# Expert routing of a one-core hybrid layer: a softmax for each head, gathers inside the routing, and a 16-bit look-up

## The chip, the cores and the metric

The kernel runs on one core of one Trainium2 chip. The metric is the device time of one execution in microseconds. Of several executions the median is taken. TensorE is PE in the profile (its weight loads PEld), VectorE is DVE, ScalarE is ACT, GpSimd is POOL and SyncE is SP.

## The reference

One layer works on 512 tokens of width 1024 with 256 context tokens. A first half (adaLN, RMSNorm, an input projection, an S5 scan and a Hyena convolution, an output projection, a gated residual) is not touched by the change. The second half is PEER, product-key retrieval of single-neuron experts. Each of 8 heads scores 128 + 128 half keys, takes the best 16 of each half, adds them in pairs, and takes the best 16 of the sums:

```python
v1, i1 = lax.top_k(s1, 16)
v2, i2 = lax.top_k(s2, 16)
cand = (v1[..., :, None] + v2[..., None, :]).reshape(..., 256)
sc, ci = lax.top_k(cand, 16)
e = take_along_axis(i1, ci // 16) * 128 + take_along_axis(i2, ci % 16)
g = jax.nn.softmax(sc, axis=-1)
act = jax.nn.gelu(einsum('chkd,cd->chk', take(u_tab, e), hb))
out = einsum('chk,chkd->cd', g * act, take(v_tab, e))
```

So each token has 8 x 16 = 128 experts e out of 16384, each with a gate g. `x + gate * out` and a final RMSNorm are the output. All data are float32.

## The kernel before, in words

The 512 tokens are served in two ways. The first 128 tokens (`NG`) are served by **gathers**: `gathered(s)` (lines 1428 to 1439) fetches for slot s (one of the 128 head-and-rank slots) each token's expert row, u and v side by side, 1 MB in all, by an indirect DMA on POOL's queue (line 1430, index column `gidx[:, s]`) into one of three buffers `uvr` (`NUV`). DVE then multiplies u with the token's row and sums (line 1431, the dot product), ACT takes the gelu of the dot (line 1434) and multiplies by the gate `gt0[:, s]` (line 1436), and DVE adds gate times v to `accg` (line 1439). The other 384 tokens (`ND`) are served **densely**: all 128 tiles of 128 experts are computed for all these tokens. For tile i, `first(i)` (lines 1360 to 1370) loads the u weights, splits them into a high part (ACT, line 302) and a low part (DVE, line 303), runs 24 matmuls of 384 columns and takes the gelu. `second(i)` (lines 1602 to 1631) loads the v weights `vr` (512 KB), splits them in the same way (`vh` on ACT, line 1611; `vl` on DVE, line 1612), multiplies the stored gelu `gal` by the stored gates `gc` (DVE, line 1617), splits the product (lines 1620 and 1621) and runs 18 matmuls of 512 columns into `pacc`.

Every dense product is three float32r matmuls (high x high, high x low, low x high: `mm3`, lines 306 to 309).

The stages in order of time, behind the untouched first half:

1. **Routing**, the loop over the 8 heads (lines 1465 to 1490): two query projections of 24 matmuls (`pq`), the scores of four token blocks (`psc`, line 1483), the best 16 of each half (`top16`, lines 1346 to 1352, on DVE), and `pairs` (lines 1382 to 1419). `pairs` adds the 54 candidate sums and, beside them, the 54 expert numbers (`ca`; `NCAND` = 54), takes the best 16 of the sums, and looks their expert numbers up: for each of four token blocks, line 1416 compares the 16 found positions with 0..53 (a 128 x 16 x 54 mask), line 1417 multiplies the mask by the 54 numbers, and line 1418 sums over the 54 to give `EID`. All three are DVE instructions on float32. Behind each head, `run_ahead(RH)` places `first` for 6.3 tiles on average, whose results go to DRAM (`GA`): they fill PE while DVE sorts. Once, behind all heads, `softmax(None)` (lines 1443 to 1455) makes the gates of all heads with one ACT exponential, and writes `gidx` and `gt0`, which the gathers need.
2. **Gates** (lines 1567 to 1590): `columns` and `gates` turn expert numbers and gates into dense gate rows for the 384 tokens, in 96 groups of four tokens, with four small matmuls a group (`pgg`). Behind each group, `gathers(G_SHARE)` adds 0.23 gathers and `run_ahead(RG)` adds 0.34 tiles. `run_ahead(RS)` puts 4 tiles ahead of it, and `run_ahead(NRUN)` the rest, up to `NRUN` tiles, behind it.
3. **The second loop** (lines 1638 to 1643): `second(i)` for all 128 tiles. For i under `NRUN` nothing else runs on PE; from there on, `first` of one tile goes with each `second`. The remaining gathers are spread over this loop by the factor `left` (line 1635), so many for an i under `NRUN` times `R_RUN`, and so many for each later i.

`gathers(share)` adds up shares and issues `gathered` whenever the sum passes a whole number; its first DVE instruction is kept behind the instruction passed as `after`. A scheduler that works from estimated times orders the instructions of each engine at build time; on the chip each engine and each DMA queue then runs strictly in that order.

Of the kernel before, what the change touches and what calls it, by code (L numbers as in the profile page):

```python
# [11 lines left out]
I32 = mybir.dt.int32  # L12
BF16 = mybir.dt.bfloat16
U32 = mybir.dt.uint32
AF = mybir.ActivationFunctionType
ALU = mybir.AluOpType
AX = mybir.AxisListType

P = 128
# [52 lines left out]
          ("bglu", 4), ("gs5", 4), ("ghy", 4), ("negt", 4), ("a_re", 32), ("a_im", 32), ("lstep", 32))  # L72
NG = 128
SG = 32
NRUN = 91
NUV = 3
G_SHARE = 0.23
R_RUN = 0.4
ACT_OH = (2,1)
RG = 0.34  # L80
RH = 6.3
RS = 4
EQ_POOL = 3
G_LAG = 3
# [7 lines left out]
QUIET = 1  # L92
WGT_ACT = 1
RGATE = 0
PERHEAD = 0
GH = 2.0
NOO = 3
S5M = 1
HYAT = 2
# [5 lines left out]
NCAND = 54 if MERGE else 50  # L105
# [123 lines left out]
def build(tc, I, out, dbg=None, stop=None):  # L229
# [58 lines left out]
    def b2(name, shape, dtype=F32):  # L288
        return cur[0].tile(shape, dtype, tag="b2", name=name, bufs=nb2[0])
# [4 lines left out]
    def sm(name, shape, dtype=F32, bufs=1, tag=None):  # L294
        return cur[0].tile(shape, dtype, tag=tag or name, name=name, bufs=bufs)

    def wblock(src, name, lo_eng=None):
# [3 lines left out]
        lo = wp.tile([P, D], F32R, tag="wl", name=name + "l")  # L301
        nc.scalar.activation(hi, raw, AF.Copy)
        (lo_eng or (nc.vector if FQ else nc.gpsimd)).tensor_tensor(lo, raw, hi.bitcast(F32), ALU.subtract)
# [30 lines left out]
    V = nc.vector  # L334
    A = nc.scalar
# [83 lines left out]
    sc = cp.tile([P, 8, 2], F32, tag="sc", name="sc")  # L419
    A.activation(sc, ccs, AF.Silu)  # L420
    mod = cp.tile([P, 48], F32, tag="mod", name="mod")
# [15 lines left out]
    def modulated(name, rows, n, scale_c, shift_c, put, ks):  # L437
        for k in ks:
# [3 lines left out]
            hi, lo = put(k)  # L442
            A.activation(hi, pp[:, :n], AF.Identity, bias=shift_c[:, k:k + 1], scale=scale_c[:, k:k + 1])
            t = b2(f"{name}t{k}", [P, 512])[:, :n]
# [3 lines left out]
    def root_sums(n, name, ps_, diag, nb=4):  # L448
# [9 lines left out]
        def inverse(scale):  # L458
            c4 = cp.tile([P, 4], F32, tag="c4", name=name + "4", bufs=2)
            A.activation(c4[:, 0:nb], pc_[:, 0:nb], AF.Sqrt, bias=epsc, scale=scale)  # L460
            V.reciprocal(c4[:, 0:nb], c4[:, 0:nb])
# [8 lines left out]
    def row_sums(n, name, ps_, tmp, width=512):  # L470
# [4 lines left out]
        def add(t, eng=None):  # L475
            i = at[0]
            at[0] += 1
            hi, lo = (tmp(f"{name}{c}{i}", F32R)[:, 0:width] for c in "hl")
            A.activation(hi, t, AF.Copy)
            (eng or V).tensor_tensor(lo, t, hi.bitcast(F32), ALU.subtract)  # L480
# [3 lines left out]
        def inverse(scale, o, view=lambda t: t):  # L484
            root = tmp(name + "q", F32)[:, 0:width]
            A.activation(root, pc_, AF.Sqrt, bias=epsc, scale=scale)
            V.reciprocal(o, view(root))
# [848 lines left out]
    gate[0] = None  # L1336
    iota50 = sm("iota50", [P, NCAND])
    GP.iota(iota50, pattern=[[1, NCAND]], base=0, channel_multiplier=0, allow_small_or_imprecise_dtypes=True)
    iotak = sm("iotak", [P, P])
    GP.iota(iotak, pattern=[[1, P]], base=0, channel_multiplier=0, allow_small_or_imprecise_dtypes=True)  # L1340
    gt0 = rt("gt0", [P, P])
# [2 lines left out]
    EID = sm("EID", [P, 4, 8, 16])  # L1344

    def top16(val, idx, src, n, name):
        V.max(val[:, 0:8], src)
        V.max_index(idx[:, 0:8], val[:, 0:8], src)  # L1348
        rest = sm(name, [P, 128], tag="rest", bufs=4)[:, :n]
        V.match_replace(rest, val[:, 0:8], src, NEG)  # L1350
        V.max(val[:, 8:16], rest)
        V.max_index(idx[:, 8:16], val[:, 8:16], rest)  # L1352
# [4 lines left out]

    GA = dram.tile([NRUN, P, ND], F32, name="GA")

# [15 lines left out]
    def run_ahead(share):  # L1375
        ran[0] += share
        while ran[1] < min(NRUN, ran[0]):
            i = ran[1]
            ran[1] += 1
            nc.scalar.dma_start(GA[i], first(i, V if QUIET else GP))  # L1380

    def pairs(hd, val, idx):

        if MERGE:
            V.tensor_copy(val[:, :, 4:8], idx)
            V.tensor_scalar(val[:, 0, 4:8], val[:, 0, 4:8], float(P), None, ALU.mult)
            ca = sm(f"ca{hd}", [P, 8, NCAND], tag="cand", bufs=2)
            cand, cid = ca[:, 0:4], ca[:, 4:8]
            at = 0
            for (i0, m, n) in RECTS:  # L1390
                V.tensor_tensor(ca[:, :, at:at + m * n].rearrange("p w (i j) -> p w i j", j=n), val[:, 1, :, 0:n].unsqueeze(2).broadcast_to((P, 8, m, n)),
                                val[:, 0, :, i0:i0 + m].unsqueeze(3).broadcast_to((P, 8, m, n)), ALU.add)
                at += m * n
        else:
            idf = sm(f"idf{hd}", [P, 2, 4, 16], tag="idf", bufs=2)
            V.tensor_copy(idf, idx)
            V.tensor_scalar(idf[:, 0], idf[:, 0], float(P), None, ALU.mult)
            cand = sm(f"cand{hd}", [P, 4, NCAND], tag="cand", bufs=2)
            cid = sm(f"cid{hd}", [P, 4, NCAND], tag="cid", bufs=2)
            at = 0  # L1400
            for i in range(9):
                n = 16 // (i + 1) if i < 8 else 8
                for (dst, s) in ((cand, val), (cid, idf)):
                    if i < 8:
                        V.tensor_tensor(dst[:, :, at:at + n], s[:, 1, :, 0:n], s[:, 0, :, i:i + 1].broadcast_to((P, 4, n)), ALU.add)
                    else:
                        V.tensor_tensor(dst[:, :, at:at + n], s[:, 0, :, 8:16], s[:, 1, :, 0:1].broadcast_to((P, 4, n)), ALU.add)
                at += n
        pos = sm(f"pos{hd}", [P, 4, 16], U32, tag="pos", bufs=2)
        for lt in range(4):  # L1410
            top16(SC[:, lt, hd], pos[:, lt], cand[:, lt], NCAND, f"rc{hd}{lt}")
        posf = sm(f"posf{hd}", [P, 4, 16], tag="posf", bufs=2)
        V.tensor_copy(posf, pos)
        for lt in range(4):
            eq = sm(f"eq{hd}{lt}", [P, 16, NCAND], tag="eq", bufs=2)
            V.tensor_tensor(eq, posf[:, lt].unsqueeze(2).broadcast_to((P, 16, NCAND)), iota50.unsqueeze(1).broadcast_to((P, 16, NCAND)), ALU.is_equal)
            (GP if not QUIET and lt < EQ_POOL else V).tensor_tensor(eq, eq, cid[:, lt].unsqueeze(1).broadcast_to((P, 16, NCAND)), ALU.mult)
            last = V.tensor_reduce(EID[:, lt, hd], eq, AX.X, ALU.add)
        return last
# [23 lines left out]
    def softmax(hd):  # L1443
        h_ = slice(hd, hd + 1) if hd is not None else slice(0, 8)
        n = 1 if hd is not None else 8
        sc, gx = SC[:, :, h_], GX[:, :, h_]
        V.tensor_tensor(gx, sc, sc[:, :, :, 0:1].broadcast_to((P, 4, n, 16)), ALU.subtract)
        A.activation(gx, gx, AF.Exp)
        gsum = sm(f"gsum{hd}", [P, 4, 8], tag="gsum", bufs=2)[:, :, 0:n]
        V.tensor_reduce(gsum, gx, AX.X, ALU.add)  # L1450
        V.reciprocal(gsum, gsum)
        V.tensor_tensor(gx, gx, gsum.unsqueeze(3).broadcast_to((P, 4, n, 16)), ALU.mult)
        c_ = slice(16 * h_.start, 16 * h_.stop)
        V.tensor_copy(gidx[:, c_], EID[:, 0, h_].rearrange("p h k -> p (h k)"))
        V.tensor_copy(gt0[:, c_], GX[:, 0, h_].rearrange("p h k -> p (h k)"))
# [3 lines left out]
    def gathers(share, after):  # L1459
        due[0] += share  # L1460
        while due[1] < min(P, due[0]):
            gathered(due[1], after)
            due[1] += 1

    for hd in range(8):
# [12 lines left out]
        val = sm(f"val{hd}", [P, 2, 8 if MERGE else 4, 16], tag="val", bufs=2)  # L1478
        idx = sm(f"idx{hd}", [P, 2, 4, 16], U32, tag="idx", bufs=2)
        for lt in range(4):  # L1480
# [5 lines left out]
        last = pairs(hd, val, idx)  # L1486
        if PERHEAD:
            softmax(hd)
            gathers(GH if hd else 0, last)
        run_ahead(RH)  # L1490

# [77 lines left out]
    for e in range(2):  # L1569
# [5 lines left out]
        A.activation(gx2[:, e * 512:(e + 1) * 512], pgx, AF.Copy)  # L1575
    if not PERHEAD:
        softmax(None)
# [7 lines left out]
    for lt in range(1, 4):  # L1585
        if RGATE:
            cols_lt = columns(lt, eids[:, lt], gts[:, lt])
        for b_ in range(P // SG):
            (gates_r if RGATE else gates)((lt - 1) * (P // SG) + b_, cols_lt if RGATE else cols[lt - 1], b_ * SG)
    run_ahead(NRUN)  # L1590
    fr.close()
# [42 lines left out]
    nc.sync.dma_start(gfin, I["g_final"].broadcast_to((P, D)))  # L1634
    left = (P - due[1] - N_SLACK) / (R_RUN * NRUN + (P - NRUN))
    ready = {}
    made = NRUN
    for i in range(P):
# [3 lines left out]
        last = second(i, ready.pop(i, None))  # L1642
        gathers(left * (R_RUN if i < NRUN else 1.0) if i < P - 1 else P, last)

# [58 lines left out]
```

## Time and profile before

| what | us |
|---|---|
| median of three runs | 1772.52 |
| the three runs | 1772.52, 1769.88, 1780.96 |
| the profiled execution, its own time | 1780.91 |
| its span (first to last instruction) | 1779.1 |
| mean granted TensorE clock in it | 0.977 of full speed |

The span is 1.8 us shorter than the execution's own time. A profile's busy time is that of one engine; matmuls are pipelined, so that the distance between the starts of two equal matmuls says more than the duration of one.

### The profile page before, as it was taken

The numbers are of one execution on the slowest core, as the hardware profiler recorded it, in microseconds if no ns is written. First come the engines' busy times: TensorE is split into PE (matmuls) and PEld (weight loads), VectorE is DVE, ScalarE is ACT, GpSimd is POOL, SyncE is SP. The second block draws the span as 40 slices with busy tenths as digits, with TensorE's granted clock in tenths as the row PEclk, the third lists the DMA queues.
The fourth block names the chain that finished last, engine by engine and source line by source line (L and its number), as shares of the span: only waits on it lengthen the run. The fifth ranks groups of instructions, "written<-read, shape, count | busy, mean of one in ns | idle before, by whom it ended". The sixth has DMA issues, their size and how long they took to land.

```text
span 1779.1 us, 24951 instructions
## 1 busy us (share of the span) xinstructions
PE 1669.7 (94%) x8731; PEld 1410.9 (79%) x8731; DVE 1489.1 (84%) x3031; ACT 817.7 (46%) x1622; POOL 165.5 (9%) x158
## 2 busy tenths in 40 slices
PE   5799998788899999999999999989999999999997
PEld 1477655365699999999999998877778778999996
DVE  7964988986788989989999966888878888788888
ACT  3443543134443223326999864443434434444444
POOL 0000000000000000001111100111111112121222
PEclk9899999898899999999999999999999999999998
DMA  9426454131434444445988899999999999999982
GB/s 373 155 88 211 162 163 101 48 75 63 136 123 149 137 146 145 145 142 214 345 330 316 320 346 380 381 384 372 364 338 377 369 349 326 329 325 353 338 322 96
DMA packets 171092, 437.31 MB, mean 246 GB/s; under 512 B 17235, under 2 KB 102868, under 8 KB 151766
## 3 DMA queue, kind: packets, MB, share of 16 engines
q1 hardware_dynamic: 129286, 251.87, 41.8%
q0 software_dynamic: 18432, 134.23, 20.1%
q10 hardware_dynamic: 23248, 49.62, 7.8%
q8 instruction: 69, 1.13, 0.3%
q14 instruction: 57, 0.47, 0.1%
HBM read 382.11 MB, written 53.51 MB: 245 GB/s over the span
## 4 chain that ended last, share of the span: by engine, by line
PE 63%; DVE 12%; DMA 1%; issue 1%; ACT 1%; SPq 0%; DVEq 0%; ACTq 0%
PE pacc L307 10%; PE pacc L308 10%; PE pacc L309 9%; PE pa L309 6%; PE pa L307 6%; PE pa L308 6%; PE pgg L1560 5%; PE pq L309 2%; PE pq L307 2%; PE pq L308 2%; DVE idx L1352 1%; DVE rs L1350 1%; PE pg L1266 1%; DVE idx L1348 1%; DMA GD<-gst 1%
## 5 line engine op out<-in xcount | busy, mean ns | idle before, releaser
L308 PE MATMUL pacc<-vl,wwh 128*128 128x512 f32 x768 | 299.2, 390 | 0.3 <-DVE vl L1612 0.3
L309 PE MATMUL pacc<-vh,wwl 128*128 128x512 f32 x768 | 292.8, 390 | 0.0
L1430 POOL DMA_INDIRECT uvr<-in_uv_dram,gidx x128 | 153.2, 1197 | 1092.1 <-DVE accg L1439 764.2
L307 PE MATMUL pacc<-vh,wwh 128*128 128x512 f32 x768 | 241.0, 393 | 13.7 <-ACT vh L1611 13.7
L1612 DVE TENSOR_TENSOR vl<-vr,vh 128x1024 fp32r<-128x1024 f32 x128 | 155.5, 1220 | 33.3 <-ACT vh L1611 33.1
L307 PEld LDWEIGHTS pacc<-vh,wwh 128*128 128x128 f32 x768 | 144.2, 189 | 45.6 <-ACT vh L1611 16.9
L308 PEld LDWEIGHTS pacc<-vl,wwh 128*128 128x128 f32 x768 | 144.3, 188 | 30.5 <-DVE vl L1612 0.7
L309 PEld LDWEIGHTS pacc<-vh,wwl 128*128 128x128 f32 x768 | 144.2, 188 | 30.0
L1439 DVE SCALAR_TENSOR_TENSOR accg<-uvr,wgt,accg 128x1024 f32<-128x1024 f32 x128 | 163.7, 1279 | 4.5 <-ACT wgt L1436 1.9
L1611 ACT ACTIVATE vh<-vr 128x1024 fp32r<-128x1024 f32 x128 | 133.2, 1049 | 53.5 <-PE pacc L309 39.9
L1431 DVE SCALAR_TENSOR_TENSOR junk<-uvr,hrow 128x1024 f32<-128x1024 f32 x128 | 155.9, 1218 | 0.0
L1620 ACT ACTIVATE wwh<-gw 128x384 fp32r<-128x384 f32 x128 | 67.1, 524 | 183.0 <-PE pacc L308 152.1
L1621 DVE TENSOR_TENSOR wwl<-gw,wwh 128x384 fp32r<-128x384 f32 x128 | 70.8, 555 | 51.8 <-ACT wwh L1620 51.8
L1560 PE MATMUL pgg<-o,o 128*128 128x128 f32 x768 | 94.6, 275 | 0.0
L1560 PEld LDWEIGHTS pgg<-o,o 128*128 128x128 f32 x768 | 93.7, 191 | 0.0
L1551 DVE TENSOR_TENSOR o<-iotak,cols 128x512 f32<-128x512 f32 x96 | 65.9, 687 | 7.8 <-PE pgg L1560 7.6
L1434 ACT ACTIVATE wgt<-dots 128x1 f32<-128x1 f32 x128 | 25.4, 198 | 102.4 <-DVE junk L1431 102.4
L1558 DVE TENSOR_SCALAR o<-iotak,cols 128x128 f32<-128x128 f32 x240 | 70.5, 345 | 0.0
L1556 ACT ACTIVATE o<-o,cols 128x128 f32<-128x128 f32 x144 | 63.8, 494 | 0.2
L1369 ACT ACTIVATE ga<-pa 128x384 f32<-128x384 f32 x128 | 60.6, 474 | 6.0 <-PE pa L309 4.5
L1562 ACT ACTIVATE gst<-pgg 128x512 f32<-128x512 f32 x96 | 57.0, 594 | 3.1 <-PE pgg L1560 2.5
L1617 DVE TENSOR_TENSOR gw<-gal,gc 128x384 f32<-128x384 f32 x91 | 50.0, 553 | 3.4 <-DMA gal<-GA 2.8
(1811 smaller groups left out, 4136.3 us busy)
## 6 DMA issues: line engine op xcount, KB each, us to landing
vr<-in_uv_dram SPq DMA_DIRECT2D x128, 512.0 KB
GD<-gst ACTq DMA_DIRECT2D x12, 2048.0 KB
gc<-GD SPq DMA_DIRECT2D x32, 768.0 KB
GA<-ga ACTq DMA_DIRECT2D x91, 192.0 KB
gal<-GA SPq DMA_DIRECT2D x91, 192.0 KB
wb<-in_w_ada_dram SPq DMA_DIRECT2D x32, 512.0 KB
wa<-in_w_ada_dram SPq DMA_DIRECT2D x8, 1024.0 KB
KD<-kk SPq DMA_DIRECT2D x16, 256.0 KB
```

Source lines behind the costliest of these rows:

```text
L307: nc.tensor.matmul(o, a[0], b[0], start=start, stop=False)
L308: nc.tensor.matmul(o, a[0], b[1], start=False, stop=False)
L309: nc.tensor.matmul(o, a[1], b[0], start=False, stop=stop_)
L1430: GP.indirect_dma_start(out=uvr, out_offset=None, in_=I["uv"], in_offset=bass.IndirectOffsetOnAxis(ap=gidx[:, s:s + 1], axis=0))
L1431: ins = V.scalar_tensor_tensor(junk, uvr[:, 0:D], 1.0, hrow, ALU.mult, ALU.mult, accum_out=dots[:, s:s + 1])
L1439: V.scalar_tensor_tensor(accg, uvr[:, D:2 * D], wgt[:, s:s + 1], accg, ALU.mult, ALU.add)
L1558: last = V.tensor_scalar(o1[:, e], iotak, cols[:, 0, t:t + 1], cols[:, 2, t:t + 1], ALU.is_equal, ALU.mult)
L1560: mm = PE.matmul(pg[:, e, :], o2[:, e], o1[:, e], start=True, stop=True)
L1611: A.activation(vh, vr, AF.Copy)
L1612: (V if QUIET or i >= P - VLV else GP).tensor_tensor(vl, vr, vh.bitcast(F32), ALU.subtract)
L1620: A.activation(wh, gw, AF.Copy)
L1621: last = V.tensor_tensor(wl, gw, wh.bitcast(F32), ALU.subtract)
```

## The change

- `PERHEAD` = 1: `softmax(hd)` runs for each head inside the routing loop, on 4 x 16 scores a token instead of 4 x 8 x 16, and writes that head's 16 columns of `gidx` and `gt0`. The call behind the loop goes.
- `GH` = 3: behind each head but the first, three gathers are placed in the routing loop.
- `PAIR16` = 1: the look-up of `pairs` works on 16-bit types. ACT makes a bf16 copy of the positions, spread out to 16 x 54 (`posx`), and an int16 copy of the expert numbers (`cid16`); DVE compares bf16 with bf16 into int16, multiplies int16 by int16, and sums int16 to float32.
- `NRUN` 91 to 96, `RH` 6.3 to 7, `R_RUN` 0.4 to 0.35.

```diff
-NRUN = 91
+NRUN = 96
-R_RUN = 0.4
+R_RUN = 0.35
-RH = 6.3
+RH = 7
-PERHEAD = 0
-GH = 2.0
+PERHEAD = 1
+GH = 3.0
+PAIR16 = 1
...
+    iota16 = sm("iota16", [P, NCAND], BF16)
+    A.activation(iota16, iota50, AF.Copy)
...
         posf = sm(f"posf{hd}", [P, 4, 16], tag="posf", bufs=2)
         V.tensor_copy(posf, pos)
+        if PAIR16:
+            cid16 = sm(f"cid16{hd}", [P, 4, NCAND], I16, tag="cid16", bufs=2)
+            A.activation(cid16, cid, AF.Copy)
+            for lt in range(4):
+                posx = sm(f"posx{hd}{lt}", [P, 16, NCAND], BF16, tag="posx", bufs=2)
+                A.activation(posx, posf[:, lt].unsqueeze(2).broadcast_to((P, 16, NCAND)), AF.Copy)
+                eq = sm(f"eq{hd}{lt}", [P, 16, NCAND], I16, tag="eq", bufs=2)
+                V.tensor_tensor(eq, posx, iota16.unsqueeze(1).broadcast_to((P, 16, NCAND)), ALU.is_equal)
+                V.tensor_tensor(eq, eq, cid16[:, lt].unsqueeze(1).broadcast_to((P, 16, NCAND)), ALU.mult)
+                last = V.tensor_reduce(EID[:, lt, hd], eq, AX.X, ALU.add)
+            return last
         for lt in range(4):
```

The loop over the heads had the two calls already, behind `if PERHEAD` (lines 1487 to 1489): `softmax(hd)` and `gathers(GH if hd else 0, last)`.

## Rows read from the trace of the kernel before

**Rows 1.** The page, first part: busy time of each engine in the span
```profile
PE 1669.7 (94%) x8731; PEld 1410.9 (79%) x8731; DVE 1489.1 (84%) x3031; ACT 817.7 (46%) x1622; POOL 165.5 (9%) x158
```

**Rows 2.** Windows: stretch; busy us (count) of PE, PEld, DVE, ACT, POOL; clock, DMA share, GB/s
```profile
510.00:825.00 315.00, 312.52 (x1726) 296.36 (x1725) 283.96 (x988) 101.18 (x137) 4.23 (x3) 1.00 0.46 151
825.00:835.00 10.00, 8.79 (x57) 8.28 (x57) 9.05 (x26) 8.64 (x25) 0.00 (x0) 1.00 0.94 383
...
1160.00:1460.00 300.00, 286.05 (x1246) 233.62 (x1245) 251.57 (x338) 121.69 (x225) 51.27 (x43) 0.99 1.02 366
1460.00:1766.00 306.00, 306.00 (x1523) 275.21 (x1522) 252.84 (x318) 132.71 (x258) 59.80 (x51) 1.00 0.85 306
```

**Rows 3.** Windows, one head of six tiles, then one of seven
```profile
549.15:587.42 38.27, 37.98 (x210) 35.71 (x209) 35.19 (x125) 11.72 (x17) 0.00 (x0) 1.00 0.44 145
...
625.69:668.26 42.57, 42.16 (x234) 39.93 (x233) 36.41 (x125) 13.15 (x19) 0.00 (x0) 1.00 0.45 148
```

**Rows 4.** Timeline of DVE, where a head begins (start, duration, idle before)
```profile
668.26 0.52 DVE L1347 MAX8 val<-psc 128x8 f32<-128x128 f32 x2 [2.99 <-PE psc L1483]
```

**Rows 5.** Groups by form, DVE, 440 to 860 us, then its end alone (busy us, mean ns)
```profile
L1416 DVE TENSOR_TENSOR eq<-posf,iota 128x864 f32<-128x864 f32 x32 | 32.6, 1050 | 0.3
L1418 DVE TENSOR_REDUCE EID<-eq 128x16 f32<-128x864 f32 x32 | 32.3, 1040 | 0.0
L1417 DVE TENSOR_TENSOR eq<-eq,ca 128x864 f32<-128x864 f32 x32 | 32.3, 1049 | 0.0
...
L1391 DVE TENSOR_TENSOR ca<-val 128x64 f32<-128x64 f32 x2 | 0.4, 220 | 0.0
```

**Rows 6.** Timeline of DVE in the first half: an instruction with one full operand
```profile
402.57 0.48 DVE L1199 TENSOR_SCALAR catz<-x2t,small 128x512 f32<-128x512 f32 x1
```

**Rows 7.** Groups by form, DVE: gates, then the second loop up to 1460 us
```profile
L1551 DVE TENSOR_TENSOR o<-iotak,cols 128x512 f32<-128x512 f32 x93 | 63.8, 687 | 7.7 <-PE pgg L1560 7.6
...
L1439 DVE SCALAR_TENSOR_TENSOR accg<-uvr,wgt,accg 128x1024 f32<-128x1024 f32 x53 | 67.8, 1280 | 2.5 <-ACT wgt L1436 0.6
L1431 DVE SCALAR_TENSOR_TENSOR junk<-uvr,hrow 128x1024 f32<-128x1024 f32 x53 | 64.5, 1218 | 0.0
...
L1617 DVE TENSOR_TENSOR gw<-gal,gc 128x384 f32<-128x384 f32 x88 | 48.3, 553 | 3.4 <-DMA gal<-GA 2.8
```

**Rows 8.** Waits of PE, routing, 510 to 825 us (the longest of eight)
```profile
PE pa L309 <- DVE u44l L303: 0.4, 1, 0.4
```

**Rows 9.** Timeline of ACT around the one softmax
```profile
806.18 1.28 ACT L1448 ACT_TABLE_LOAD   x1
...
807.48 0.63 ACT L1448 ACTIVATE GX<-GX 128x512 f32<-128x512 f32 x1
```

**Rows 10.** Timeline of PE in the second loop, starts of two iterations
```profile
1160.36 1.52 PE L307 MATMUL pacc<-vh,wwh 128*128 128x512 f32 x6
...
1164.44 1.52 PE L307 MATMUL pacc<-vh,wwh 128*128 128x512 f32 x6
```

**Rows 11.** Waits of PE, 1160 to 1460 us (total, times, longest)
```profile
PE pacc L307 <- ACT vh L1611: 13.7, 7, 3.6
```

**Rows 12.** Windows of the second loop, columns as in rows 2
```profile
1200.00:1300.00 100.00, 93.61 (x409) 76.24 (x409) 85.61 (x116) 39.53 (x76) 18.60 (x16) 0.99 1.02 364
1300.00:1400.00 100.00, 98.40 (x428) 80.53 (x427) 82.60 (x112) 40.89 (x75) 17.30 (x14) 0.99 0.99 362
1400.00:1500.00 100.00, 98.67 (x444) 82.30 (x443) 84.77 (x112) 43.07 (x79) 17.00 (x15) 1.00 0.97 342
```

**Rows 13.** The page: POOL's queue (packets, MB, share), then sizes of DMA issues
```profile
q0 software_dynamic: 18432, 134.23, 20.1%
...
vr<-in_uv_dram SPq DMA_DIRECT2D x128, 512.0 KB
...
gc<-GD SPq DMA_DIRECT2D x32, 768.0 KB
...
gal<-GA SPq DMA_DIRECT2D x91, 192.0 KB
```

More of the change, by code (lines that the diff above doesn't have):

```diff
@@ L14 @@
 U32 = mybir.dt.uint32
+I16 = mybir.dt.int16
 AF = mybir.ActivationFunctionType
```

## The prediction

> **What bounds the kernel now.** I read the page first: PE is busy for 94% of the span, DVE for 84% [rows 1]. Such shares are averages, so next come the windows by stage [rows 2]. PE is busy for 312.52 of 315 us in the routing and for all of 306 us in the last part of the second loop. The stretches with idle time that the change can reach are three: 2.5 us in the routing, 1.2 us at the change to the gates, and 14.0 us (300 - 286.05) between 1160 and 1460 us of the second loop. Nothing in the change removes a matmul. So what it can win is that idle time, some 17.7 us of 1779 or 1.0%, and what it can lose is new idle time of PE in the routing, where DVE gets more to do.
>
> The windows of single heads say how near DVE is to being the bound there [rows 3]. A head with six tiles takes 38.27 us and one with seven 42.57, with PE busy but for 0.3 to 0.4 us in both: a tile costs 4.30 us of PE, and a head lasts as long as its PE work. DVE is idle for 6.16 us of a seven-tile head (42.57 - 36.41), 2.99 of them in a single wait for the next head's scores [rows 4].
>
> In the second loop the waits name one cause for PE: seven waits for `vh`, 13.7 us in all [rows 11]. An iteration without `first` takes 4.08 us (1164.44 - 1160.36) [rows 10]. It moves 512 KB of `vr`, 192 KB of `gal` and a quarter of 768 KB of `gc` [rows 13], 0.918 MB, and its part of a gather of 134.23 / 128 = 1.049 MB [rows 13]. With 23 gathers placed before the loop (96 groups x 0.23, rounded up), `left` is (128 - 23 + 7) / (0.4 x 91 + 37) = 1.526, so 0.610 gathers an iteration: 1.558 MB in 4.08 us, or 382 GB/s. The windows show 1.02 as DMA share in this part and 0.85 in the last part, where PE never waits [rows 2]. The loop is thus held by PE and, for its first 91 iterations, by the DMA engines as well.
>
> **The change, part by part.** *Five more tiles ahead.* 6.3 x 8 = 50.4, so 51 tiles in the routing, become 56; `first` leaves the second loop five times (37 to 32). At 4.30 us a tile the routing gets 21.5 us longer and the loop 21.5 us shorter: no net effect while PE stays busy. The last three tiles behind the gates stay three (88 to 91 before; 92.64 is rounded up to 93, then 96). The five added splits take DVE time in the routing and give it back in the loop; a seven-tile head [rows 3] holds them already.
>
> *Three gathers a head.* 7 x 3 = 21 gathers move ahead. Each costs DVE 1.218 + 1.280 us [rows 7], so 7.5 us a head. DMA has room in the routing: 151 GB/s at a share of 0.46 [rows 2], and three gathers in 42.57 us add 74 GB/s. Their transfers need not be late: once two heads have written 32 columns of `gidx`, three buffers can be filled well before DVE wants them. Behind a gather that waits for its column or its buffer POOL has only gathers; SP's queue is passed by none of the moved work, and ACT's issues five more stores of 192 KB.
>
> *Softmax by head.* Six small DVE instructions a head. On 64 numbers the nearest row takes 0.22 us [rows 5]: 1.3 us a head, with 0.8 (if the shorter ones are cheaper) and 2 as bounds. On ACT each head adds two table loads of 1.28 us [rows 9], a short exponential, four spread copies of 864 elements (0.63 us for 512 [rows 9], so at most 1.06 in proportion; I take 0.95) and the small ones of three gathers: some 8 us, where ACT is busy for 13.15 of 42.57 us [rows 3]. This is covered as long as ACT's in-order queue does not hold up a tile's high part.
>
> The table load is where a rule speaks against the change. The row shows the exponential starting 1.30 us after the load's start [rows 9]. The Trainium skill (ScalarE: Activation LUTs, What ACT_TABLE_LOAD costs) puts a switch of table sets at about 2.66 us, since a drain follows the load; 16 switches would then be 43 us of ACT in place of 21. The trace does not show the drain at this place.
>
> *The look-up in 16 bits.* The compare and the multiply take 1.05 us each, four times a head [rows 5]. No row shows a 16-bit operand on DVE. If time goes by elements, the cost stays 1.05; if by bytes, 864 elements of two bytes are 1728 bytes a partition, between the rows of 384 and 512 float32 elements, 0.553 and 0.687 us [rows 7]: about 0.60. Both rows are equally near. I take 0.60, because one row shows that bytes count: 512 elements with one full operand take 0.48 us [rows 6], with two 0.687 [rows 7]. That saves 8 x 0.45 = 3.6 us a head; the sum stays at 1.04. The ends, 0 and 4.0 us, are kept for the range. The Trainium skill (VectorE: DVE Perf Modes, The perf-mode tier table) gives `tensor_tensor` double rate on 16-bit data in SBUF and `tensor_reduce` none; an estimate by that page is 0.61 us for each of the two, and no run here shows it yet.
>
> *Sum for the routing.* DVE in a head: 36.41 + 7.5 + 1.3 - 3.6 = 41.6 us, against 42.57 us of PE's head. DVE stays just below PE, with 1 us of slack in place of 6.2. PE's waits for DVE's low parts are 0.4 us or less now [rows 8], 0.3 us a head; with so little slack I take 0.9, which adds 0.6 x 8 = 5 us. At the change to the gates the look-up behind the last head shrinks by 3.6 us and the softmax of eight heads is gone; of PE's 1.2 us of idle time there I take 1 as won.
>
> *The second loop.* 44 gathers lie ahead of it (21 + 22.08, rounded up); `left` is (128 - 44 + 7) / (0.35 x 96 + 32) = 1.387, and 0.485 gathers an iteration: 1.427 MB in 4.08 us, 350 GB/s. DVE has 0.125 x 2.5 = 0.3 us less an iteration. Stretches with 342 and 362 GB/s lost 1.33 and 1.60 us of PE in 100 us, the one with 364 lost 6.39 [rows 12]. At 350 I take 1.5: over 96 iterations of 4.08 us that is 5.9 us, so 14.0 - 6 = 8 us are won. Bounds: nothing, or all 14.
>
> The net is +5 - 1 - 8 = -4 us. Against the profiled execution's own 1780.9 us that gives 1776.9. This execution was 8.4 us above the median of the three runs; I apply the difference to the median: **1768.5, say 1768 us**, and within 1% of before, which is about what a measurement of this kernel can tell from no change.
>
> **The rivals.**
>
> *A. DVE becomes the bound of the routing (slower).* Place: seven heads with gathers. If 16-bit operands bring nothing, DVE has 45.2 us of work a head, 2.6 more than PE; it decides from the point where DVE's work passes 42.57 us. Over seven heads that is 18 us if DVE fills all its waits, and 39 if it keeps the wait for scores of 2.99 us [rows 4] as well; half way, 28. In place of the 5 us: 1772.5 + 28 - 1 - 8 = 1791. For it: no 16-bit row, and a wait that comes once a head now. Against it: gathers are just the work that could fill that wait.
>
> *B. The waits for `vh` stay.* They may come from the order of ACT's queue, in which `vh` stands behind the two small gather activations, and not from full DMA engines. Then only the routing changes: 1772.5 + 5 - 1 = 1776. For it: the wait ends with ACT. Against it: no such wait after 1460 us, with more gathers an iteration.
>
> *C. All idle time goes.* DVE keeps up without new waits, and both the 14.0 and the 2.5 us vanish: 1772.5 - 17 = 1755.5. Against it: even 342 GB/s lost 1.33 us in 100 [rows 12].
>
> *D. ACT holds up the tiles.* Two table loads and an exponential that waits for DVE, in order ahead of a high part; if each load costs PE its 1.28 us, 16 x 1.28 = 20 us, in place of the 5: 1772.5 + 20 - 9 = 1784. Against it: PE's only wait in the stretch of the one softmax was for a low part, under 0.4 us [rows 8]. By the page named above the price would double; the row speaks for the lower one.
>
> **How the numbers follow.** Forecast 0.44, A 0.18, B 0.15, C 0.15, D 0.08. The range goes from C's 1756 to 1787: it holds the forecast, B and D, half of C and the lighter third of A, and leaves out 0.08 + 0.11 = 0.19. Faster by over 1% is below 1754.8: half of C and a little, 0.10. Slower by over 1% is above 1790.2: the heavier part of A, with a little of D, 0.13. Within 1%: 0.77.
>
> **What would show it.** Right: a routing of some 340 us (8 x 42.57) with PE busy above 97%, the two 16-bit instructions near 0.60 us, the sum near 1.04, 21 gathers before the gates; in the second loop DMA near 350 GB/s and PE's waits for `vh` below 7 us. Wrong: heads of over 43.5 us with PE waiting for low parts (A) or for high parts behind a table load (D); waits for `vh` of 13 us as before (B); or compare and multiply at 1.05 us.

## The result and the profile after

The changed kernel takes 1753.62 us (median of four runs, 1749.34 to 1755.15) against 1772.52 before: a ratio of 0.988 [0.9858, 0.9902], 1.2% faster. The forecast was 1768, its low end 1756. Rival C, "all idle time goes", had 1755.5.

The page of the changed kernel, busy time of each engine in a span of 1747.6 us (own time 1749.34), answers to [rows 1]:

```profile
PE 1662.0 (95%) x8731; PEld 1409.3 (81%) x8731; DVE 1464.7 (84%) x3073; ACT 868.9 (50%) x1686; POOL 168.5 (10%) x158
```

PE's share rose by one point and its work did not change (8731 matmuls in both), so the shares say almost nothing. The time must be cut at points that both kernels have: the first scores matmul, the first matmul of the second loop and the last one. Windows of the kernel before, cut there (stretch; its length, then busy us and count of PE, PEld, DVE, ACT and POOL; clock, DMA share, GB/s):

```profile
501.30:1081.80 580.50, 574.90 (x3510) 557.58 (x3511) 514.59 (x1464) 320.30 (x668) 32.02 (x26) 1.00 0.64 227
1081.80:1766.40 684.60, 670.65 (x3125) 575.17 (x3123) 568.88 (x742) 286.31 (x540) 123.68 (x104) 1.00 0.94 341
```

The same windows of the changed kernel:

```profile
492.00:1089.50 597.50, 595.27 (x3633) 579.45 (x3634) 544.11 (x1574) 382.43 (x780) 62.49 (x47) 1.00 0.73 262
1089.50:1735.50 646.00, 645.15 (x3002) 553.29 (x3000) 516.17 (x676) 275.92 (x494) 96.17 (x83) 1.00 0.92 327
```

Behind the first half the time fell from 1265.1 to 1243.5 us, by 21.6. Five tiles moved forward, and three matmuls of a sixth: 123 matmuls (3633 - 3510). By rows 3 a tile of 24 matmuls is 4.18 us of busy PE (42.16 - 37.98), so 21.4 us moved from the second window to the first. Without them the first window gained 4.4 us (580.5 + 21.4 - 597.5) and the loop 17.2 (684.6 - 21.4 - 646.0). PE's idle time (length less busy) went from 5.6 to 2.2 us and from 13.95 to 0.85: 16.5 us together. The other 5.1 us are PE's busy time, with the same 6635 matmuls; they are taken up in the last section. The first half, which the change does not touch, took 501 us in the one profile and 492 in the other; over the profiles of all runs it lies between 489.5 and 501.3 us, so the medians (18.9 us apart) and the windows need not agree to the microsecond.

Waits of PE in the changed kernel's loop, 1060 to 1760 us (total, times, longest), and, by windows, the stretch of [rows 2, 11] and one head of seven tiles, as in [rows 3]:

```profile
PE pacc L309 <- ACT wwh L1635: 0.8, 1, 0.8
```

```profile
552.52:594.49 41.97, 41.97 (x234) 39.94 (x233) 40.52 (x140) 20.77 (x32) 4.29 (x3) 1.00 0.64 224
...
1160.00:1460.00 300.00, 300.00 (x1325) 248.03 (x1324) 244.66 (x328) 124.89 (x217) 41.04 (x36) 1.00 1.00 355
```

The seven waits for `vh` are gone and PE works 300.00 of 300 us, although the DMA share is still 1.00. In a head DVE is busy for 40.52 of 41.97 us and PE for all of it. (The second loop's lines are 15 later than before: `vh` is line 1626, `gathered` 1443 to 1454.)

The new look-up: groups by form of DVE, 440 to 860 us, as in [rows 5] (busy us, mean ns | idle before):

```profile
L1427 DVE TENSOR_REDUCE EID<-eq 128x16 f32<-128x864 int16 x32 | 33.5, 1046 | 0.2
...
L1425 DVE TENSOR_TENSOR eq<-posx,iota 128x864 int16<-128x864 bf16 x32 | 19.3, 603 | 4.6 <-ACT posx L1423 4.6
L1426 DVE TENSOR_TENSOR eq<-eq,cid 128x864 int16<-128x864 int16 x32 | 19.2, 601 | 0.0
```

The compare and the multiply fell from 1.05 to 0.60 us, the sum stayed at 1.05. The Trainium skill (VectorE: DVE Perf Modes, The perf-mode tier table) gives `tensor_tensor` twice its float32 rate on 16-bit data and `tensor_reduce` no gain. The trace agrees: 603 and 601 ns, against the prediction's estimate of 0.61 us by that page, and 1046 ns.

The softmax of one head: timeline of ACT, 600 to 607 us, as in [rows 9]:

```profile
600.20 1.28 ACT L1463 ACT_TABLE_LOAD   x1
...
601.49 0.26 ACT L1463 ACTIVATE GX<-GX 128x64 f32<-128x64 f32 x1
...
604.09 1.05 ACT L304 ACTIVATE wq6h<-wq6r 128x1024 fp32r<-128x1024 f32 x1
605.15 1.28 ACT L1373 ACT_TABLE_LOAD   x1
606.45 0.49 ACT L1373 ACTIVATE ga<-pa 128x384 f32<-128x384 f32 x1
```

Each of the two loads holds ACT up for 1.29 to 1.30 us (601.49 - 600.20, 606.45 - 605.15). The 2.66 us a switch in the Trainium skill (ScalarE: Activation LUTs, What ACT_TABLE_LOAD costs) do not show here. No wait of PE in the routing stands behind a table load: rival D is out.

### The profile page after: what moved, and what is told of

Same layout as the page of the kernel before. It is cut to its first block, busy times and chain, and to the rows that moved or that the text cites. A ratio compares the mean times of both kernels' runs of the same rounds, so it can differ in the third digit from the quotient of the medians.

```text
span 1747.6 us, 25104 instructions
## 1 busy us (share of the span) xinstructions
PE 1662.0 (95%) x8731; PEld 1409.3 (81%) x8731; DVE 1464.7 (84%) x3073; ACT 868.9 (50%) x1686; POOL 168.5 (10%) x158
## 4 chain that ended last, share of the span: by engine, by line
PE 71%; DMA 3%; DVE 3%; ACT 1%; issue 1%; SPq 0%; ACTq 0%; DVEq 0%
PE pacc L309 10%; PE pacc L310 10%; PE pacc L311 10%; PE pa L309 9%; PE pa L311 9%; PE pa L310 9%; PE pgg L1575 5%; PE pq L309 2%; PE pq L310 2%; PE pq L311 2%; DMA gal<-GA 1%; PE pg L1268 1%; PE psc L1498 1%; DMA X1R<-xrow 1%; DMA GD<-gst 1%
## 5 line engine op out<-in xcount | busy, mean ns | idle before, releaser
L311 PE MATMUL pacc<-vh,wwl 128*128 128x512 f32 x768 | 297.4, 390 | 0.0
L309 PE MATMUL pacc<-vh,wwh 128*128 128x512 f32 x768 | 232.4, 389 | 0.8 <-ACT wwh L1635 0.8
L1566 DVE TENSOR_TENSOR o<-iotak,cols 128x512 f32<-128x512 f32 x96 | 65.8, 686 | 12.8 <-PE pgg L1575 12.8
```

Source lines behind the costliest of these rows:

```text
L309: nc.tensor.matmul(o, a[0], b[0], start=start, stop=False)
L311: nc.tensor.matmul(o, a[1], b[0], start=False, stop=stop_)
```

## The experiments

Two questions were open. Why did the loop lose nearly all its waits, and not only 8 of 14 us? And why did the routing win, with DVE at 97% (40.52 of 41.97)?

### The loop: bytes, DVE work or the order of the queues

**Half the bytes, the same instructions** (on the kernel before):

```diff
+out["u1"] = cc(u)
...
-uvr = rt(f"uvr{s}", [P, 2 * D], ...)
-GP.indirect_dma_start(out=uvr, ..., in_=I["uv"], ...)
+uvr = rt(f"uvr{s}", [P, D], ...)
+GP.indirect_dma_start(out=uvr, ..., in_=I["u1"], ...)
...
-V.scalar_tensor_tensor(accg, uvr[:, D:2 * D], ...)
+V.scalar_tensor_tensor(accg, uvr[:, 0:D], ...)
```

> The kernel before with every gather fetching only the u half of a row, 0.52 MB instead of 1.05; the second DVE instruction of a gather reads that same half, so all instructions of DVE and ACT stay as many and as long. Left out: the v half of the gathered experts. Theory DMA (PE's waits for vh come from full DMA engines): 1.24 MB an iteration, about 303 GB/s, and the waits of PE in the second loop fall from 17 us to under 3; the time is 15 us or more below the kernel before. Theory order (they come from gather instructions ahead of vh in the queues of DVE and ACT): the waits stay at 12 to 20 us and the time within 5 us of before.

Measured: 1752.5 us, 0.9877 [0.9852, 0.9902]. Its window:

```profile
1160.00:1460.00 300.00, 300.00 (x1328) 248.74 (x1327) 260.47 (x353) 131.02 (x239) 46.57 (x46) 1.00 0.90 297
```

No wait for `vh` is left, with more DVE work than in the changed kernel (260.47 us against 244.66), and the ratio is that of the whole change. But the build also gave ACT, DVE and PE another order of instructions (ahead of the loop, for one, lie 27 matmuls of tiles fewer). So this run alone does not say whether the bytes or the order did it.

**Less DVE work, the same bytes** (on the kernel before):

```diff
-V.scalar_tensor_tensor(junk, uvr[:, 0:D], 1.0, hrow, ...)
+V.scalar_tensor_tensor(junk[:, 0:P], uvr[:, 0:P], 1.0, hrow[:, 0:P], ...)
-V.scalar_tensor_tensor(accg, uvr[:, D:2 * D], wgt[:, s:s + 1], accg, ...)
+V.scalar_tensor_tensor(accg[:, 0:P], uvr[:, D:D + P], wgt[:, s:s + 1], accg[:, 0:P], ...)
```

> The kernel before with the two DVE instructions of each gather cut to 128 of 1024 columns (about 0.3 us each instead of 1.2); bytes, DMAs and ACT instructions unchanged. Left out: seven eighths of the dot products and of the weighted sums of the first 128 tokens. Theory DMA: 382 GB/s are still asked for, the waits for vh stay above 10 us and the time within 6 us of before. Theory order: DVE has 1.2 us less an iteration, the waits fall under 3 us and the time by 15 us or more.

Measured: 1781.42 us, 1.0042 [1.0028, 1.0055]. Its window, and PE's waits in the loop:

```profile
1160.00:1460.00 300.00, 283.85 (x1219) 230.94 (x1218) 172.22 (x327) 118.75 (x218) 42.48 (x41) 0.98 1.00 355
```

```profile
PE pacc L307 <- ACT vh L1611: 18.8, 10, 2.7
```

DVE's busy time fell to 172 of 300 us and the waits did not shrink. They do not come from the amount of DVE's work.

**How many gathers a head** (on the changed kernel; the value is the only edit): 0, 2 and 4 in place of 3.

```diff
-GH = 3.0
+GH = 0.0
```

> The changed kernel with no gathers in the routing (three a head to none); all 105 that are left after the gates then fall in the second loop, 0.597 an iteration instead of 0.485. Theory 1 (the win is the relief of the second loop): PE's waits for vh are back, 12 to 18 us, and the time is 1767 to 1773. Theory 2 (the win is the tiles run ahead, the softmax by head or the routing): below 1758.

```diff
-GH = 3.0
+GH = 2.0
```

> The changed kernel with two gathers a head: 14 in the routing, 0.523 an iteration of the second loop, 359 GB/s asked for. If the win is the bytes taken out of the loop, its waits lie between those of none a head (17.2 us in the profile) and of three (0.8): 3 to 10 us, and the time 4 to 14 us above the changed kernel. If any gathers in the routing do it (because gathers are then prefetched at the start of the gates, say): no waits, within 3 us of the changed kernel.

```diff
-GH = 3.0
+GH = 4.0
```

> The changed kernel with four gathers a head instead of three. DVE's work of a head goes from 40.5 to 43.0 us and passes PE's 42.0. Theory 1 (the slack of DVE in the routing sets how many gathers it takes): heads of 43 us or more or a late start of the gates, 5 to 12 us above the changed kernel, since the second loop has nothing left to win (0.8 us of waits). Theory 2 (DVE is not near its bound): within 3 us of the changed kernel.

The table has, for each, what an iteration without `first` asks for (worked out as in the prediction: 0.918 MB and 0.35 x `left` gathers of 1.049 MB in 4.08 us), PE's waits in the loop and how many of them are for `vh`, the tiles ahead of the loop (its `pa` matmuls by 24), the length of the two windows cut as above, what follows the last matmul to the span's end, and the ratio to the kernel before on the same chip:

| gathers a head | asked, GB/s | waits | for `vh` | tiles ahead | before the loop | loop | behind it | ratio |
|---|---|---|---|---|---|---|---|---|
| before (none, R_RUN 0.4) | 382 | 13.9 | 7 | 93.9 | 580.6 | 684.5 | 12.8 | 1 |
| 0 | 379 | 17.2 | 9 | 99 | 598.3 | 668.6 | 26.9 | 1.0071 [1.0048, 1.0094] |
| 2 | 359 | 8.7 | 4 | 99 | 598.5 | 656.9 | 12.3 | 0.9925 [0.989, 0.9959] |
| 3, the change | 350 | 0.8 | 0 | 99 | 597.5 | 645.9 | 12.2 | 0.988 [0.9858, 0.9902] |
| 4 | 340 | 1.8 | 1 | 100 | 608.9 | 643.1 | 12.1 | 0.994 [0.9913, 0.9966] |

Without gathers in the routing the waits are back, in the changed kernel too; here are PE's waits in its loop for none and for two:

```profile
PE pacc L309 <- ACT vh L1626: 14.1, 9, 3.3
PE pacc L309 <- ACT wwh L1635: 1.6, 1, 1.6
PE pacc L310 <- DVE vl L1627: 1.5, 2, 0.7
```

```profile
PE pacc L309 <- ACT vh L1626: 5.3, 4, 1.3
PE pacc L309 <- ACT wwh L1635: 2.7, 1, 2.7
PE pacc L310 <- DVE vl L1627: 0.7, 1, 0.7
```

The waits for `vh` get fewer as the loop asks for less. The other runs fit: at 382 GB/s the two with short DVE work and with 16 bits alone have 10 and 12, at 379 the one with the tiles alone has 9, at 352 the two with gathers alone and with six tiles one each, at 350 the one in float32 two. With no gathers in the heads, more was lost than expected, and the rest lies at the end. With `R_RUN` at 0.35 and nothing fetched early, the last gather is issued 4 us ahead of the last matmul (timeline of POOL and PE), where the kernel before issues it 23 us ahead and the changed kernel 54 (1681.49, last matmul 1735.42):

```profile
1753.30 1.68 POOL L1445 DMA_INDIRECT uvr<-in_uv_dram,gidx  x1 [0.79 <-DVE accg L1454]
...
1757.45 0.39 PE L311 MATMUL pacc<-vh,wwl 128*128 128x512 f32 x1
```

With four gathers one tile more (4.2 us) lies ahead of the loop. Without it the part before the loop is 7.2 us longer than with three, and the loop 1.4 us longer too. A head's DVE work (42.8 to 44.0 us in the heads with gathers) comes to lie above PE's 42.0, and these heads last 43.4 to 47.2 us.

**What PE's waits for `vh` wait for.** A wait that falls with the rate asked looks like a load that comes late. The traces say otherwise. Here are ACT's two largest waits in the kernel before, 1127 to 1468 us:

```profile
ACT wwh L1620 <- PE pacc L308: 139.1, 74, 4.7
ACT wgt L1434 <- DVE junk L1431: 64.4, 40, 3.5
```

The three smaller ones are for DVE and PE as well; none is for a DMA. Around PE's first wait, which ends at 1178.17, ACT does this:

```profile
1176.65 0.52 ACT L1620 ACTIVATE wwh<-gw 128x384 fp32r<-128x384 f32 x1 [1.25 <-PE pacc L308]
1177.08 1.99 ACT L1611 ACTIVATE vh<-vr 128x1024 fp32r<-128x1024 f32 x2
```

The first of the two `vh` is that of iteration 21 (counted from 0), and its `vr` had landed at 1171.11, 6.0 us earlier (the last landing mark of that DMA in the trace). But in ACT's order it stands behind `wwh` of iteration 23. There are three buffers for `wwh` (`NVH` = 3), so that one cannot start until PE is done with iteration 20. Then `vh` takes its 1.04 us, and PE stands still for 1.33.

This holds for every such wait. In the fourteen profiles, from iteration 9 on, `vh` of an iteration stands behind the `wwh` of the second one after it in 65 places, and PE waits at 63 of them (the other two are iteration 88 of the kernel before, where `first` gives PE other work). At none of the other places does PE wait for `vh`. In all 63 `vr` had landed before `vh` began, by 5.5 to 8.6 us in the kernel before and by 0.8 to 10.8 over all runs. The half-bytes run and the changed kernel have no such place; in both of them each `vh` of the stretch without `first` stands behind the `wwh` of its own or the next iteration at most. The longest waits (2.7 to 3.6 us) are those where a gather's gelu, waiting for DVE, stands ahead of `vh` too. One wait is of another kind: in six profiles PE waits in iteration 4 for a `wwh` (0.8 us in the changed kernel, up to 2.7 in the others), and there ACT had stood still until a `vr` landed.

So the waits for `vh` are made when the program is built, by the order in ACT's queue, and not by the DMA engines on the chip. How many there are goes with the bytes that the loop asks for; that the scheduler's estimated times count these bytes fits all runs, but no run shows its estimates. An edit that moves `vh` ahead in ACT's queue, and nothing else, was not run.

### The routing: what the 16-bit look-up and the tiles are for

**The look-up in float32** (on the changed kernel):

```diff
-PAIR16 = 1
+PAIR16 = 0
```

> The changed kernel with the look-up back on float32 (16-bit off). Theory 1 (the routing absorbs the gathers only because the 16-bit look-up gave DVE room): DVE's work of a head goes from 40.5 to about 44.1 us and passes PE's 42.0, heads last 44 to 45 us, PE waits in the routing, and the time is 15 to 25 us above the changed kernel, 1769 to 1778. Theory 2 (the room was there anyway): 1751 to 1757.

Measured: 1767.99 us, 0.9944 [0.9926, 0.9961], so 14 us above the changed kernel by the medians, and 11 by the ratios (0.9944 against 0.988). The part before the loop is 15.0 us longer (612.5) and the loop 1.7 shorter (644.2); one tile more lies ahead, so by work it is 10.8 us longer before the loop and 2.5 in it. The mark of a head on DVE (the first cast of `pairs`), from its timeline, comes every 44.9 us in the mean of the six heads with gathers (43.8 to 46.2), for example:

```profile
558.50 0.23 DVE L1389 CAST val<-idx 128x128 f32<-128x128 uint32 x1
...
603.79 0.23 DVE L1389 CAST val<-idx 128x128 f32<-128x128 uint32 x1
...
649.47 0.22 DVE L1389 CAST val<-idx 128x128 f32<-128x128 uint32 x1
```

In the changed kernel it is 41.97:

```profile
552.52 0.23 DVE L1389 CAST val<-idx 128x128 f32<-128x128 uint32 x1
...
594.49 0.23 DVE L1389 CAST val<-idx 128x128 f32<-128x128 uint32 x1
```

PE stays busy in most of the heads' time: it is idle for 4.0 us in all seven together, and a window of 42 us in the middle has no idle time.

```profile
636.00:678.00 42.00, 42.00 (x234) 40.09 (x234) 41.43 (x138) 16.69 (x24) 1.13 (x2) 1.00 0.58 205
```

DVE falls behind by some 3 us a head (44.9 - 42.0) while PE still has tiles to run; the longest of PE's new waits stands at the change to the gates (`pgg` for `o`, 3.9 us). By windows PE is idle for 10.5 us before the loop (612.50 - 601.99) where the changed kernel has 2.2. This is rival A's mechanism, at half its price.

**The look-up in 16 bits alone** (the changed kernel with all else set back; `PAIR16` stays 1, and `GH` acts only with `PERHEAD`):

```diff
-NRUN = 96
-R_RUN = 0.35
-RH = 7
+NRUN = 91
+R_RUN = 0.4
+RH = 6.3
...
-PERHEAD = 1
+PERHEAD = 0
```

> The kernel before with the 16-bit look-up alone. DVE has 3.6 us less work a head, but PE sets the length of a head: both theories expect 1770 to 1775, unless the small waits of PE for DVE's low parts (2.5 us in the routing) go, which is at most 3 us. Below 1767 would say that DVE held the routing before.

A miss: 1787.76 us, 1.0057 [1.0037, 1.0076]. A head of seven tiles got shorter, and PE has no idle time in it any more (0.4 us before [rows 3]):

```profile
630.60:672.50 41.90, 41.90 (x234) 39.98 (x233) 33.00 (x126) 16.71 (x23) 0.00 (x0) 1.00 0.45 150
```

But the part before the loop did not (581.3 us, against 580.6), and the loop took 698.7 us against 684.5, with 16.7 us of waits for `vh` in twelve waits. The edit touches nothing in that loop; the scheduler ordered the loop's instructions otherwise. Of the 14.2 us, 3.3 are 19 matmuls of tiles that moved into the loop, 6.5 are idle time of PE, and 4.4 are PE's busy time behind the waits.

**The gathers and the softmax by head alone**, in float32 (on the kernel before):

```diff
-PERHEAD = 0
-GH = 2.0
+PERHEAD = 1
+GH = 3.0
```

> The kernel before with softmax by head and three gathers a head alone (float32 look-up, 6.3 tiles a head, 91 ahead). DVE's work of a six-tile head is 35.2 + 7.5 + 1.3 = 44.0 us against 38.3 of PE. Theory 1: the routing is bound by DVE, heads of about 44 us, +40 us there, about -16 in the second loop: 1790 to 1800. Theory 2 (room anyway): 1755 to 1760.

Measured: 1781.12 us, 1.0027 [1.001, 1.0044], between the two. The loop wins 10.3 us (674.2) and keeps 1.5 us of waits; the part before it loses 21.5 (602.1). By work it is 14.0 and 25.2, since 21 matmuls of tiles (3.7 us) moved into the loop. PE's waits, 480 to 860 us, two rows of them:

```profile
PE ptr L1505 <- DVE ef L1503: 11.9, 1, 11.9
...
PE pgg L1560 <- ACT o L1556: 3.7, 1, 3.7
```

DVE's lag again, at the change to the gates. With 51 tiles in eight heads there is less PE time in which DVE can do the gathers.

**The tiles ahead alone** (on the kernel before):

```diff
-NRUN = 91
-R_RUN = 0.4
-RH = 6.3
+NRUN = 96
+R_RUN = 0.35
+RH = 7
```

> The kernel before with 96 tiles ahead, seven a head, and 0.35 alone (no gathers in the routing, one softmax, float32 look-up). Per iteration of the second loop 0.597 gathers and in its last part 1.7. If tiles ahead win nothing by themselves and only the gathers' place counts: like the changed kernel without head gathers, a ratio of 1.004 to 1.01 to the kernel before. If the tiles ahead are what won: a ratio of 0.99.

Measured: 1792.37 us, 1.0101 [1.0079, 1.0124]. The tiles themselves are nearly neutral (601.8 and 666.9 us, 1268.7 against 1265.1; of these 3.6 us 2.8 are waits in the loop, 16.8 against 14.0). What makes it slower lies behind the last matmul: 26.7 us instead of 12.8. The last gather is issued at 1762.50, 4 us ahead of the last matmul, as without gathers in the heads above. The two runs with these settings and no gathers in the heads show it, and none of the others, in which the last gather is issued 23 us ahead or more.

**Everything but the tiles** (on the changed kernel, the same three constants set back):

```diff
-NRUN = 96
-R_RUN = 0.35
-RH = 7
+NRUN = 91
+R_RUN = 0.4
+RH = 6.3
```

> The changed kernel with 6.3 tiles a head, 91 ahead and 0.4, so the softmax by head, the gathers and the 16-bit look-up alone. DVE's work of a head is about 40 us against 38.3 (six tiles) to 42 us (seven) of PE. If DVE sets the routing there, it falls behind by 1 to 2 us in most heads and PE waits at the change to the gates: 5 to 12 us above the changed kernel. If the tiles a head do not matter: within 3 us of it.

Measured: 1767.01 us, 0.9959 [0.9941, 0.9977]. Six tiles fewer lie ahead of the loop (93 against 99), so the part before it should be 572.4 us (597.5 - 25.1) and the loop 671.0 (645.9 + 25.1); they are 587.6 and 672.4, so nearly all of the loss lies ahead of the loop. PE waits again for ACT and DVE in the routing and at the change to the gates, 480 to 860 us:

```profile
PE pgg L1575 <- DVE ei L1515: 3.0, 1, 3.0
PE pa L309 <- ACT ga L1373: 1.8, 3, 0.7
```

### Both kernels once more

Neither is edited; both ran on one chip.

> The kernel before once more, for the length of its untouched first half (501.3 us to the first scores in the first profile, 492.0 in that of the changed kernel). If that difference is only from run to run, this profile has another length, anywhere from 490 to 500 us, with the waits of the second loop again at 15 to 20 us. If the change shortens the first half, it is 499 to 503 us again.

> The changed kernel once more, as the measure for the others: a ratio of 0.986 to 0.990 to the kernel before, no waits above 1 us in the second loop.

Measured: 1772.81 us for the kernel before, in a single run, and 1755.89 for the changed one, 0.9876 [0.9835, 0.9916]. From the first scores to the last matmul they take 1265.1 and 1245.2 us (1265.1 and 1243.4 in the first pair), with 13.9 and 1.3 us of waits in the loop (15 to 20, and none above 1, were expected). Their first halves took 493 and 501 us, the other way round than in the first pair: the gain does not come from there.

## Why the prediction was wrong

In the profiles, the forecast of +4 us before the loop (+5 and -1) and -8 in it came out as -3.4 and -13.1 us of PE's idle time, and 5.1 us of PE's busy time went as well: -21.6 against -4, or -18.9 by the medians. All signs that the prediction named for being right came (heads full of PE, 0.60 and 1.05 us, 355 GB/s, waits under 7 us). They could not tell the forecast from rival C.

**Where the idle time was: right; what caused it: wrong.** The prediction named the waits for `vh`, and held that the loop is held "for its first 91 iterations, by the DMA engines as well". In every wait of the kernel before, `vr` had landed 5.5 to 8.6 us before its `vh` began, and between 1127 and 1468 us ACT waited for no DMA. A DMA share of 1.02 stood beside the waits and did not make them: the changed kernel shows 1.00 and works 300.00 of 300 us. The cause is rival B's, the order of ACT's queue, though mostly with a later `wwh` ahead of `vh` and not the gather's two activations alone. What B had wrong is that the order would stay: moving the gathers gave a new one without these places.

**How much of it goes: wrong.** The step read: "Stretches with 342 and 362 GB/s lost 1.33 and 1.60 us of PE in 100 us ... At 350 I take 1.5". Measured were 0.8 and 1.3 us in the whole loop, in place of 5.9, so 13.1 us of idle time went and not 8. A price by the DMA rate had no ground, since the waits do not come from it. Nor were the three windows of rows 12 three rates: 91 iterations of 4.08 us from 1081.8 on, with 14 us of waits, end at 1081.8 + 371 + 14, about 1467 us (in the trace, 1468.0). So up to there all three windows hold iterations that asked 382 GB/s, and the third has some 33 us of the stretch behind, where nothing waits, at 306 [rows 2]. Its 342 GB/s is a mean over two kinds of iteration, and its 1.33 us belong to the fast one.

**The routing: wrong in sign, and the largest error (7.4 us).** "with so little slack I take 0.9, which adds 0.6 x 8 = 5 us". PE's idle time before the loop fell from 5.6 to 2.2 us, and a head is all PE (41.97 of 41.97). A larger busy share of DVE did not make PE wait more: DVE went from 86% of a head [rows 3] to 97%, and PE waited less. The run with 16 bits alone has no idle time in its heads either, so the small waits of before go with the float32 look-up. That PE's low parts had stood behind it in DVE's order is likely and was not followed up. The terms under it held: DVE's sum came to 40.52 us a head (41.6 forecast), and 16 bits to 0.60 us. ACT's 8 us were 7.6 (20.77 - 13.15).

**Rival A: refuted here, true one step away.** With float32 DVE is the bound, and that costs 11 to 14 us, not 28; A's time was 1791, and the run's ratio of 0.9944 is 1763 on the same scale. The price took the lag of seven heads in full as time of PE; but PE had tiles to run while DVE lagged. Of the 13.2 us by windows, 8.3 are idle time before the loop (10.5 - 2.2), 1.9 idle time in it, and 3.0 PE's busy time.

**Neutral tiles and D: right.** Five tiles more ahead cost 3.6 us by themselves (1268.7 against 1265.1 us in the run with them alone), most of it waits in the loop, and no wait of PE stands behind a table load.

**The range.** C was held for 0.15 because "even 342 GB/s lost 1.33 us", the misreading above, and the low end was put at C's own time of 1756, with no room for its spread. C came nearest: it priced 17 us of idle time, and 16.5 went. The reckoning was also short of one part, in C as in the forecast: "what it can win is that idle time", some 17.7 us, left out the slower matmuls behind the waits.

**What remains open.** The change is several edits that need each other: each alone is slower (1.0057, 1.0027, 1.0101), together they are faster. For the gathers, the 16 bits and the tiles, the need is shown by leaving each out of the changed kernel; the softmax by head was not left out by itself, since the gathers in the heads need its columns. Why the build puts `vh` late in one program and not in another was not read from the scheduler. Each edit also gives a new order of the whole kernel, so a single edit's result here holds that as well.

## What to carry to other kernels

When an engine waits for a copy or a split, look at when the load landed and at what stands ahead of the copy in its engine's queue, before blaming a full DMA. Here a DMA share of 1.00 to 1.02 went with 14 us of waits and with 0.8, and at every wait for `vh` the load had landed. Asking 8% fewer bytes of the loop (382 to 350 GB/s) gave a program without the late places, while one third less DVE work did not. To price a wait from a trace, compare windows that lie wholly in one kind of iteration. When an edit moves work between stages, count what moved before comparing their lengths. An engine that takes work from another stage must be given the time first (16 bits and seven tiles a head), and the last transfer must still be issued well before the last use (4 us cost a longer end, 23 us did not).

## What the runs showed of the hardware

A short wait of PE can cost more than its length. In the kernel before (timeline of PE), six matmuls take 1.52 us without a wait [rows 10], 1.66 us behind a wait of 1.33 us, and 2.93 behind one of 3.63:

```profile
1178.17 1.66 PE L307 MATMUL pacc<-vh,wwh 128*128 128x512 f32 x6 [1.33 <-ACT vh L1611]
...
1299.39 2.93 PE L307 MATMUL pacc<-vh,wwh 128*128 128x512 f32 x6 [3.63 <-ACT vh L1611]
```

Windows ahead of the longer wait's end, behind it, and later:

```profile
1295.70:1299.30 3.60, 0.06 (x1) 0.00 (x0) 3.04 (x5) 1.80 (x5) 0.94 (x1) 0.94 1.01 298
1299.40:1302.30 2.90, 2.90 (x7) 2.32 (x8) 2.90 (x4) 1.84 (x2) 1.68 (x1) 0.51 1.07 386
1302.40:1306.00 3.60, 3.60 (x17) 2.95 (x16) 1.23 (x2) 1.07 (x2) 0.00 (x0) 1.00 1.02 378
```

PE stood still for 3.6 us, then the granted clock was 0.51 (the level of 1.2 GHz) for 2.9 us, then 1.00. The run with short DVE instructions repeats it: a wait of 2.70 us, then a clock of 0.58 over 2.6 us. It does not come every time: behind the wait of 3.30 us of the kernel before the clock stayed at 1.00, and the six matmuls took 1.66 us. So a wait that goes gives back its own time and that of any slow matmuls behind it. Of the 5.1 us of PE's busy time that went, 4.1 lie in the loop (670.65 - 21.4 - 645.15); the long wait alone has about 1.4 of them (2.93 - 1.52), and the rest was not divided among the others.
